# Batch normalisation over 512 MB: the first tile's split moved from a half to a quarter of its columns

## The chip, the cores and the metric

The kernel runs on one core of a Trainium2 chip. Its time is the device time of one execution in microseconds; where several runs were made, the median stands for them. One profiled execution gives the trace from which all details are read. Lower is better.

## The reference

```python
eps = 1e-5
mean = running_mean.reshape(1, -1, 1, 1)
var = running_var.reshape(1, -1, 1, 1)
gamma = gamma.reshape(1, -1, 1, 1)
beta = beta.reshape(1, -1, 1, 1)
return gamma * (x - mean) / np.sqrt(var + eps) + beta
```

`x` is 32 x 256 x 128 x 128 in fp32, 537 MB; the four parameter vectors have one value for each of the 256 channels. The output has the size of `x`. So the kernel reads 537 MB, writes 537 MB, and does one multiplication and one addition for each element.

## The kernel before

A tile is one image's block of 128 channels: 128 partitions by 128 x 128 = 16384 columns, 64 KiB a partition, 8 MB in all. There are 64 tiles (32 images by 2 channel blocks), and three buffers of that size in SBUF that the tiles take in turn. Each tile is computed in place: a load brings it in, VectorE multiplies by a scale and adds a shift for each partition (line 122), a store takes it out.

Three queues of instructions set the order of the work, all written out by hand.

- SyncE (SP) issues all loads. First the left part of tile 0 (line 84), then the four parameter vectors (line 87), then the right part of tile 0 (line 91), then tiles 1 to 63 whole (line 94). The loads of tiles 1 and 2 wait for nothing. From tile 3 on the load of tile i waits until the store of tile i - 3 has landed, since it takes that buffer.
- VectorE first turns the parameters round and works out scale and shift (lines 99 to 117; one square root of it is on ScalarE, line 107). Then it computes tile 0 in two pieces, each when its part has landed (lines 135 and 136), and tiles 1 to 62 in one piece each (line 139). Of the last tile it computes 9216 columns (line 143), and ScalarE the other 7168 beside it (line 145).
- ScalarE (ACT) issues the stores (line 133), one for each tile, when `done` says that the tile is computed. Store 0 waits for both pieces of tile 0.

Loads and stores of a tile have 128 rows of 64 KiB, one a partition. In SP's queue nothing stands between one tile's load and the next, and in ACT's queue, after the parameters' square root, there are only the stores and the last tile's piece of computation.

Of the kernel before, what the change touches and what calls it, by code (L numbers as in the profile page):

```python
# [1 line left out]

# [4 lines left out]


NBUF = 3

VCOLS = 9216


@with_exitstack
def kernel(
    ctx: ExitStack,
    tc: tile.TileContext,
    x: bass.AP,
    gamma: bass.AP,
    beta: bass.AP,  # L20
    running_mean: bass.AP,
    running_var: bass.AP,
    out: bass.AP,
):
    nc = tc.nc
    eps = 1e-5
    f32 = mybir.dt.float32

    N, C, H, W = x.shape
    P = nc.NUM_PARTITIONS  # L30
    assert C % P == 0
    NCB = C // P
    HW = H * W
    NT = N * NCB
    B = 32
    NQ = P // B
    NE = 16
    NPAR = 4

    xr = x.rearrange("n (cb p) h w -> (n cb) p (h w)", p=P)  # L40
    outr = out.rearrange("n (cb p) h w -> (n cb) p (h w)", p=P)

    params = ctx.enter_context(tc.tile_pool(name="params", bufs=1))
    data = ctx.enter_context(tc.tile_pool(name="data", bufs=1))
    bufs = [data.tile([P, HW], f32, name=f"t{s}", tag=f"t{s}") for s in range(NBUF)]
    rows = params.tile([B, NPAR * C], f32, name="rows", tag="rows")
    turned = params.tile([B, NPAR * C], f32, name="turned", tag="turned")
    par = params.tile([P, NPAR, NCB], f32, name="par", tag="par")
    eps_t = params.tile([P, 1], f32, name="eps_t", tag="eps")
    std_t = params.tile([P, NCB], f32, name="std_t", tag="std")  # L50
    rstd_t = params.tile([P, NCB], f32, name="rstd_t", tag="rstd")
    scale_t = params.tile([P, NCB], f32, name="scale_t", tag="scale")
    ms_t = params.tile([P, NCB], f32, name="ms_t", tag="ms")
    shift_t = params.tile([P, NCB], f32, name="shift_t", tag="shift")

    loaded = [tc.alloc_semaphore(f"loaded{s}") for s in range(NBUF)]
    stored = [tc.alloc_semaphore(f"stored{s}") for s in range(NBUF)]
    early = tc.alloc_semaphore("early")  # L60
    done = tc.alloc_semaphore("done")
    fetched = tc.alloc_semaphore("fetched")
    vec = tc.alloc_semaphore("vec")
    act = tc.alloc_semaphore("act")

    with tc.tile_critical():  # L66
        count = [0]

        def step(inst, sem=None, value=None):

            if sem is not None:
                inst._wait_ge(sem, value)
            elif count[0]:
                inst._wait_ge(vec, count[0])
            inst.then_inc(vec, 1)
            count[0] += 1
            return count[0]

        left, right = slice(0, HW // 2), slice(HW // 2, HW)
        last = NT - 1  # L80

        nc.sync.dma_start(out=bufs[0][:, left], in_=xr[0][:, left]).then_inc(early, 16)
        zeroed = step(nc.vector.memset(rows[:], 0.0))  # L85
        for r, ap in enumerate((running_var, gamma, beta, running_mean)):
            inst = nc.sync.dma_start(out=rows[0:NE, r * C : (r + 1) * C], in_=ap.partition_broadcast(NE))  # L87
            if r == 0:
                inst._wait_ge(vec, zeroed)
            inst.then_inc(fetched, 16)  # L90
        nc.sync.dma_start(out=bufs[0][:, right], in_=xr[0][:, right]).then_inc(loaded[0], 16)
        for i in range(1, NT):
            s, turn = i % NBUF, i // NBUF
            inst = nc.sync.dma_start(out=bufs[s][:], in_=xr[i]).then_inc(loaded[s], 16)
            if turn:
                inst._wait_ge(stored[s], 16 * turn)


        step(nc.vector.memset(eps_t[:], eps))  # L99
        step(nc.vector.transpose(out=turned[:], in_=rows[:]), fetched, 16 * NPAR)  # L100

        blocks = turned.rearrange("p (rc q b) -> p rc q b", q=NQ, b=B)
        flat = par.rearrange("p r cb -> p (r cb)")
        for q in range(NQ):
            placed = step(nc.vector.tensor_copy(out=flat[q * B : (q + 1) * B], in_=blocks[:, :, q, 0]))  # L105
        var_t, gamma_t, beta_t, mean_t = (par[:, r] for r in range(NPAR))
        nc.scalar.activation(  # L107
            out=std_t[:],
            in_=var_t,
            func=mybir.ActivationFunctionType.Sqrt,  # L110
            bias=eps_t[:],
            scale=1.0,
        )._wait_ge(vec, placed).then_inc(act, 1)
        step(nc.vector.reciprocal(out=rstd_t[:], in_=std_t[:]), act, 1)  # L114
        step(nc.vector.tensor_mul(out=scale_t[:], in0=gamma_t, in1=rstd_t[:]))  # L115
        step(nc.vector.tensor_mul(out=ms_t[:], in0=mean_t, in1=scale_t[:]))  # L116
        ready = step(nc.vector.tensor_sub(out=shift_t[:], in0=beta_t, in1=ms_t[:]))  # L117
        nc.vector.wait_ge(vec, ready)

        def compute(i, cols=slice(0, HW)):  # L120
            t, cb = bufs[i % NBUF], i % NCB
            return nc.vector.tensor_scalar(  # L122
                out=t[:, cols],
                in0=t[:, cols],
                scalar1=scale_t[:, cb : cb + 1],
                scalar2=shift_t[:, cb : cb + 1],
                op0=mybir.AluOpType.mult,
                op1=mybir.AluOpType.add,
            ).then_inc(done, 1)

        def store(i, after):
            s = i % NBUF
            nc.scalar.dma_start(out=outr[i], in_=bufs[s][:])._wait_ge(done, after).then_inc(stored[s], 16)  # L133

        compute(0, left)._wait_ge(early, 16)
        compute(0, right)._wait_ge(loaded[0], 16)
        store(0, 2)
        for i in range(1, last):
            compute(i)._wait_ge(loaded[i % NBUF], 16 * (i // NBUF + 1))
            store(i, i + 2)  # L140

        turns = last // NBUF + 1
        compute(last, slice(0, VCOLS))._wait_ge(loaded[last % NBUF], 16 * turns)
        t, cb = bufs[last % NBUF], last % NCB
        nc.scalar.activation(  # L145
            out=t[:, VCOLS:],
            in_=t[:, VCOLS:],
            func=mybir.ActivationFunctionType.Identity,
            bias=shift_t[:, cb : cb + 1],
            scale=scale_t[:, cb : cb + 1],  # L150
        )._wait_ge(loaded[last % NBUF], 16 * turns).then_inc(done, 1)
        store(last, last + 3)

        for s in range(NBUF):
            nc.sync.wait_ge(stored[s], 16 * ((NT - s + NBUF - 1) // NBUF))


# [1 line left out]
_INS = ['x', 'gamma', 'beta', 'running_mean', 'running_var']  # L159
_OUTS = [((32, 256, 128, 128), 'float32')]  # L160


# [23 lines left out]
```

## Time and profile before

| What | Value |
|---|---|
| Median of 5 runs | 2507.07 us |
| The five runs | 2515.58, 2483.45, 2509.15, 2483.73, 2507.07 us |
| The profiled execution | 2514.05 us |
| Its span, first to last instruction | 2512.3 us |
| VectorE busy | 564.0 us, 22% |
| DMA, mean over the span | 427 GB/s |
| Read and written | 536.94 MB and 536.87 MB |
| A tile on VectorE (16384 columns) | 8.81 us |
| Half of tile 0 on VectorE (8192 columns) | 4.55 us |
| Store 0 issued | 28.3 us after the start |
| Last store issued, and its time to landing | 2489.8 us, 20.7 us |

The page of a profile lists each engine's busy time, and then the span in 40 equal slices, each with a digit for the busy share in tenths. A line of a group or of the timeline reads: start, duration, engine, line of the code, operation, output<-inputs, shapes; in square brackets the time that the engine stood idle before it and what ended that. A letter q after an engine's name (SPq, ACTq) marks the queue that issues transfers; the time that such an issue takes is not the transfer's. "DMA to landing" is from the issue until the whole transfer has arrived. q1 and q10 are the DMA queues of loads and of stores.

### The profile page before, as it was taken

To read this page: it belongs to the slowest core of one execution; us is meant where nothing else is said; L and a number is where in the kernel's file an instruction comes from. 1 tells how busy PE (TensorE), PEld (TensorE's weight loads), DVE (VectorE), ACT (ScalarE), POOL (GpSimd) and SP (SyncE) were. 2 spreads that over 40 slices of the span, in tenths; PEclk is the share of its full clock that TensorE was granted. 3 is DMA by queue.
4 is the path that set the end of the run, shared out by engine and by line. 5 is a ranking of instruction groups with operands and counts; after the bars stand their busy time and mean duration, and the time that the engine had idled before them with its cause. 6 is when DMAs were issued, how large, how long until landed. Compare 5 with 4: busy or idle time off the path is not lost.

```text
span 2512.3 us, 266 instructions
## 1 busy us (share of the span) xinstructions
DVE 564.0 (22%) x76; ACT 7.9 (0%) x3; POOL 0.2 (0%) x4
## 2 busy tenths in 40 slices
DVE  3121221212212122121221212212222121221221
ACT  0000000000000000000000000000000000000001
POOL 0000000000000000000000000000000000000000
DMA  9999999999999999999999999999999999999997
GB/s 418 432 430 434 434 431 431 433 434 430 432 434 428 432 430 429 431 425 434 429 427 431 432 429 433 428 429 433 433 423 426 426 430 422 428 429 433 430 433 334
DMA packets 18707, 1073.84 MB, mean 427 GB/s; under 512 B 2128, under 2 KB 2192, under 8 KB 2192
## 3 DMA queue, kind: packets, MB, share of 16 engines
q1 hardware_dynamic: 9488, 536.94, 50.0%
q10 hardware_dynamic: 9216, 536.88, 49.6%
q14 instruction: 3, 0.02, 0.0%
HBM read 536.94 MB, written 536.87 MB: 427 GB/s over the span
## 4 chain that ended last, share of the span: by engine, by line
another core or an unknown queue 76%; DVE 22%; DMA 1%; ACT 0%; issue 0%; SPq 0%; ACTq 0%; DVEq 0%
DVE t L122 22%; DMA t<-in_x_dram 1%; ACT t L145 0%; SPq L87 0%; DVE rows L85 0%; ACTq L133 0%; DVE eps_t L99 0%; DVEq L181 0%; SPq L66 0%
## 5 line engine op out<-in xcount | busy, mean ns | idle before, releaser
L122 DVE TENSOR_SCALAR t<-t,scale_t,shift_t 128x16384 f32<-128x16384 f32 (+2 forms) x65 | 560.5, 8624 | 1910.3 <-DMA t<-in_x_dram 1910.1
L145 ACT ACTIVATE t<-t,shift_t,scale_t 128x7168 f32<-128x7168 f32 x1 | 6.4, 6361 | 2466.5 <-DMA t<-in_x_dram 2466.5
L100 DVE STREAM_TRANSPOSE turned<-rows 32x1024 f32<-32x1024 f32 x1 | 1.2, 1233 | 12.3 <-DMA rows<-in_running_mean_dram 12.3
L107 ACT ACT_TABLE_LOAD x1 | 1.3, 1283 | 0.9 <-SPq L66 0.9
L85 DVE MEMSET rows<- 32x1024 f32 x1 | 0.9, 912 | 1.2 <-SPq L66 1.2
L105 DVE COPY par<-turned 32x8 f32<-32x8 f32 x4 | 0.6, 162 | 0.1
L107 ACT ACTIVATE std_t<-par,eps_t 128x2 f32<-128x2 f32 x1 | 0.3, 295 | 14.4 <-DVE par L105 14.4
L114 DVE RECIPROCAL rstd_t<-std_t 128x2 f32<-128x2 f32 x1 | 0.2, 165 | 0.4 <-ACT std_t L107 0.4
L117 DVE TENSOR_TENSOR shift_t<-par,ms_t 128x2 f32<-128x2 f32 x1 | 0.2, 161 | 0.0
L116 DVE TENSOR_TENSOR ms_t<-par,scale_t 128x2 f32<-128x2 f32 x1 | 0.2, 160 | 0.0
L115 DVE TENSOR_TENSOR scale_t<-par,rstd_t 128x2 f32<-128x2 f32 x1 | 0.2, 160 | 0.0
L170 POOL MEMSET const-bfloat16-1.0<- 128x1 bf16 x1 | 0.1, 101 | 0.0
L170 POOL MEMSET const-uint8-127<- 128x1 uint8 x1 | 0.1, 101 | 0.0
L170 POOL MEMSET const-float32-0.0<- 128x1 f32 x1 | 0.1, 98 | 0.2 <-issue 0.2
L170 POOL MEMSET const-float32-1.0<- 128x1 f32 x1 | 0.1, 98 | 0.0
L99 DVE MEMSET eps_t<- 128x1 f32 x1 | 0.1, 59 | 0.1
## 6 DMA issues: line engine op xcount, KB each, us to landing
t<-in_x_dram SPq DMA_DIRECT2D x2, 4096.0 KB, 16.3
out_dram<-t ACTq DMA_DIRECT2D x64, 45.3
t<-in_x_dram SPq DMA_DIRECT2D x63, 63.3
rows<-in_running_var_dram SPq DMA_DIRECT2D x1, 16.0 KB, 11.2
rows<-in_gamma_dram SPq DMA_DIRECT2D x1, 16.0 KB, 11.1
rows<-in_beta_dram SPq DMA_DIRECT2D x1, 16.0 KB, 10.9
rows<-in_running_mean_dram SPq DMA_DIRECT2D x1, 16.0 KB, 11.0
```

The source lines that it names most:

```text
L85: zeroed = step(nc.vector.memset(rows[:], 0.0))
L99: step(nc.vector.memset(eps_t[:], eps))
L100: step(nc.vector.transpose(out=turned[:], in_=rows[:]), fetched, 16 * NPAR)
L105: placed = step(nc.vector.tensor_copy(out=flat[q * B : (q + 1) * B], in_=blocks[:, :, q, 0]))
L107: nc.scalar.activation(out=std_t[:], in_=var_t, func=mybir.ActivationFunctionType.Sqrt, bias=eps_t[:], scale=1.0,)._wait_ge(vec, placed).t ...
L114: step(nc.vector.reciprocal(out=rstd_t[:], in_=std_t[:]), act, 1)
L115: step(nc.vector.tensor_mul(out=scale_t[:], in0=gamma_t, in1=rstd_t[:]))
L116: step(nc.vector.tensor_mul(out=ms_t[:], in0=mean_t, in1=scale_t[:]))
L117: ready = step(nc.vector.tensor_sub(out=shift_t[:], in0=beta_t, in1=ms_t[:]))
L122: return nc.vector.tensor_scalar(out=t[:, cols], in0=t[:, cols], scalar1=scale_t[:, cb : cb + 1], scalar2=shift_t[:, cb : cb + 1], op0=myb ...
L145: nc.scalar.activation(out=t[:, VCOLS:], in_=t[:, VCOLS:], func=mybir.ActivationFunctionType.Identity, bias=shift_t[:, cb : cb + 1], scale ...
L170: nc = _bacc.Bacc("TRN2", target_bir_lowering=False, num_devices=1)
```

## The change

The boundary between tile 0's left and right part goes from column 8192 to column 4096. The left part then has a quarter of the columns (2 MB), the right part three quarters (6 MB). The names `left` and `right` are used by the two loads of tile 0 and by its two computations; nothing else is touched. Store 0 still takes the whole tile after both.

```diff
-        left, right = slice(0, HW // 2), slice(HW // 2, HW)
+        left, right = slice(0, HW // 4), slice(HW // 4, HW)
         last = NT - 1
```

## The prediction

> **What bounds the kernel now.** I read the page first: its DMA lines, then the slices.
>
> ```profile
> DVE 564.0 (22%) x76; ACT 7.9 (0%) x3; POOL 0.2 (0%) x4
> ...
> DMA  9999999999999999999999999999999999999997
> ...
> q1 hardware_dynamic: 9488, 536.94, 50.0%
> q10 hardware_dynamic: 9216, 536.88, 49.6%
> ```
>
> VectorE works 22% of the span, while the loads (q1) and the stores (q10) together fill 99.6% of the time of 16 DMA engines. The chain of waits is of little use here: it books 76% as an unknown queue, which is the time in which the tile loads run. So I went to single tiles. In the order of time VectorE's idle stretch before each tile is the load period less 8.81 us:
>
> ```profile
> 288.95 8.81 DVE L122 TENSOR_SCALAR t<-t,scale_t,shift_t 128x16384 f32<-128x16384 f32 x1 [30.02 <-DMA t<-in_x_dram]
> ...
> 1034.01 8.81 DVE L122 TENSOR_SCALAR t<-t,scale_t,shift_t 128x16384 f32<-128x16384 f32 x1 [30.85 <-DMA t<-in_x_dram]
> 1074.19 8.81 DVE L122 TENSOR_SCALAR t<-t,scale_t,shift_t 128x16384 f32<-128x16384 f32 x1 [31.36 <-DMA t<-in_x_dram]
> ```
>
> An early tile takes 38.8 us, these later ones 39.7 and 40.2. The table of stretches says the same for early, middle and end:
>
> ```profile
> 94.58:366.42 271.84, 61.68 (x7) 0.00 (x0) 0.00 (x0) 1.00 1.00 433
> 366.42:2444.39 2077.97, 467.05 (x53) 0.00 (x0) 0.00 (x0) 1.00 1.00 430
> 2475.00:2490.00 15.00, 5.08 (x1) 6.36 (x1) 0.00 (x0) 1.00 0.27 118
> ```
>
> Columns: stretch, length, VectorE, ScalarE and GpSimd busy, clock, DMA share, GB/s. Seven tiles at 38.83 us, then 53 at 39.21 us. In the third row most DMA engines have run out of work, and a few slow ones still bring in the last tile.
>
> **The floor.** In the trace's packet records a 64 KiB row takes 2.418 us at the median on its DMA engine. Each of 16 engines has 64 tiles x 8 rows x 2 directions = 1024 rows: 2476.0 us. Some 2.5 us at the start, 2 us at the end and 1.7 us around the span (2514.05 less 2512.3) make 2482. The two fastest of the five runs, 2483.45 and 2483.73 us, are practically there; the other three (2507 to 2516) and the profiled one carry about 30 us of packets over 2.418 us on the slowest engine. There are two regimes, and the clean one has been seen with the kernel as it is.
>
> **What tells the regimes apart.** A store is issued when its tile is computed; the previous store is then still running. How long it runs on I call the reserve of the store queue. From single store issues with their landings: store 0 is issued at 28.3 and lands 44.2 later, at 72.5; store 1 is issued at 64.4, so the reserve is 8.1 us.
>
> ```profile
> L133 ACTq DMA_DIRECT2D out_dram<-t x1: 374/374/374, 28.3 to 28.3; - x1
> DMA to landing us min/median/max: 44.2/44.2/44.2
> ...
> L133 ACTq DMA_DIRECT2D out_dram<-t x1: 338/338/338, 64.4 to 64.4; - x1
> DMA to landing us min/median/max: 47.3/47.3/47.3
> ```
>
> Worked the same way it is 8.3 at store 2, 7.6 at store 9, 6.6 at store 10, and from store 15 to the end between 5.6 and 7.2, with 5.6 again and again as its lowest. While it is over 7.5 the stores land every 38.7 us; after that tiles take 39.2. The landing is that of the slowest engine: fast engines end the old store some 4 us earlier, so at a reserve of 5.6 their rings are close to empty before the new store's packets are there.
>
> [...] the packet records, strung end to start into 16 sequences (they name no engine), mostly alternate between loads and stores. [...] The rows of 8192 and 16384 columns (4546 and 8812 ns) give 0.521 ns a column[...].
>
> **The change part by part.** Instructions, bytes and semaphores stay in number. The left load goes from 4 to 2 MB, the right one from 4 to 6; rows of 32 KiB become 16 and 48 KiB, two a partition as before.
>
> Parameters: their four loads are behind the left load in SP's queue and landed at 14.5, right after it (13.8). With 2 MB less ahead at some 430 GB/s they land about 4.9 us earlier, near 9.6. From there the transpose to the last small operation takes 3.2 us and the left computation 8812 - 12288 x 0.521 = 2.41 us: done by about 15.5 instead of 22.3. Nothing waits for that, since the right load lands at 23.7 as before (the same bytes ahead of it). Worth nothing; if the cover were gone it would cost at most the 2.4 us.
>
> Right computation: 12288 columns, 4.546 + 4096 x 0.521 = 6.68 us in place of 4.54. Store 0 is issued at 23.75 + 6.68 = 30.45, 2.13 us later than now. ACT's queue has nothing but later stores behind it. VectorE's next work is tile 1 at 55 us. The DMA engines do not idle: loads 1 and 2 were issued at 4.4 and 4.9 us, and the load queue runs alone for those 2.13 us. Direct cost: nothing.
>
> Phase: in 2.13 us alone each engine brings 0.88 more load rows before stores begin to take every second turn. Load 1 therefore lands 2.13 us earlier (53.4), store 1 is issued at 62.3, and store 0 lands 2.13 us later (74.6). The reserve of the store queue goes from 8.1 to 12.4 us. The price is on the load side: load 63 is issued at 2420.0 and load 62 lands at 2444.4, a reserve of 24.4 us, which falls to 20.1. Still plentiful for the slowest engine.
>
> What the reserve is worth: from 94.6 (load 2) to 2483.4 (load 63) there are 61 periods of 39.16 us. At 38.7 they would take 28 us less: 2514.05 - 28 = 2486. Against the median of 2507.07 that is 21 us, 0.8%. Early on the reserve shrank by 0.1 us a tile, then lost 1 us at one tile; from 12.4 there is room for that several times over. At the tail, the last store now starts when VectorE and ScalarE are done (2489.8), about when store 62 is (2490.6); with the larger reserve store 62 sets this alone, worth within 0.5 us either way.
>
> Unknown is whether reserve causes the regime or shows it. Bound on the good side: the floor, 2482. On the bad side there is no row for other phases between reads and writes; the worst single periods here are 40.2 us. I take the clean stretch's period.
>
> **The rivals.** (1) The reserve is only a symptom: slow read packets put the slowest engine back, whatever the phase. For it: at tile 10 the late load came before the small reserve, and several engines were slow at once. Then the regime falls as before, mostly 2502 to 2516, about 2508. (2) It helps for a time: from store 2 to 15 the reserve fell 0.21 us a tile, so 12.4 lasts some 28 tiles before 6.6 in place of 8; 20 tiles at 0.46 us are 9 us: 2498. (3) Slower: the smaller load reserve. In those sequences the fastest engines finish their loads near 2456, some 27 us ahead of the slowest: more than the 24.4 us of load reserve, so they already wait at the issue of line 94. With 20 us this begins at a smaller lead; engines then run dry and start again together, and first packets of a tile, where most of the slow packets lie, collide more. If that doubles the excess of 0.46 us a tile it costs 28 us, 2535 to 2542; if all periods become the worst seen it is 65 us. It decides once the lead passes 20 us. Against it: the early engines are level. (4) The change doesn't move the store: excluded but for a reserve that steps in whole packets (0 or 4.8 us), which ends in rival 1.
>
> **How the numbers follow.** The clean regime (2482 to 2490, forecast 2486): 0.43. Partial help (2490 to 2502): 0.20. No help (2502 to 2516): 0.20. Slower (2516 and up): 0.17, of which 0.13 past 2532. One per cent, about what a measurement of this kernel can tell from no change, is 25 us: 2482.0 and 2532.1. The floor lies at the first, so faster by over 1% gets 0.08, all from the clean regime; same 0.79; slower 0.13. The range 2481 to 2518 leaves out little but the slower rival.
>
> **What would show it.** Store 0 issued at 30.4 to 30.5; load 1 landed near 53.4; a reserve of 12 to 13 us at store 1, which stays above 7.5; idle stretches before VectorE's tiles of 29.8 to 30.1 all along; some 433 GB/s in the middle stretch. If the reserve is large and the periods are still 39.2 us, my cause is wrong and rival 1 holds. If the reserve has gone back to 5.6 by half way, rival 2. If periods pass 39.5 us on average and engines go idle before 2400 us, rival 3.

## The result, and the profile after

The changed kernel takes 2506.31 us, the median of 28 runs (2483.08 to 2509.45); the kernel before, beside it, 2502.07 us (47 runs, 2483.42 to 2525.60). The ratio is 1.0014, with a 95% interval of 0.9993 to 1.0036: no change. (Ratios, here and below, weigh the runs of both kernels; they are not those of the medians.) The profiled execution has a span of 2498.9 us (2500.64 with what lies around it).

So 2486 was wrong, and rival 1 (no help, about 2508) is what happened. Yet nearly every step on the way to it came as forecast. The order of time at the start, changed kernel (start, length, instruction, idle time before it):

```profile
23.81 6.68 DVE L122 TENSOR_SCALAR t<-t,scale_t,shift_t 128x12288 f32<-128x12288 f32 x1 [8.75 <-DMA t<-in_x_dram]
30.52 31.51 ACTq L133 DMA_DIRECT2D out_dram<-t  x2
52.84 8.81 DVE L122 TENSOR_SCALAR t<-t,scale_t,shift_t 128x16384 f32<-128x16384 f32 x1 [22.36 <-DMA t<-in_x_dram]
```

The right part takes 6.68 us, store 0 is issued at 30.5, load 1 has landed at 52.8. The first two stores, one issue each:

```profile
L133 ACTq DMA_DIRECT2D out_dram<-t x1: 376/376/376, 30.5 to 30.5; - x1
...
DMA to landing us min/median/max: 44.6/44.6/44.6
...
L133 ACTq DMA_DIRECT2D out_dram<-t x1: 339/339/339, 61.7 to 61.7; - x1
...
DMA to landing us min/median/max: 52.6/52.6/52.6
```

Store 0 lands at 75.1, store 1 is issued at 61.7: a reserve of 13.4 us, where 12.4 was worked out. Counted like this, from landings, it also stays. The page's list of transfers gives the median time of a store to its landing:

```profile
t<-in_x_dram SPq DMA_DIRECT2D x1, 6144.0 KB, 19.8
t<-in_x_dram SPq DMA_DIRECT2D x1, 2048.0 KB, 7.5
out_dram<-t ACTq DMA_DIRECT2D x64, 49.8
```

49.8 us, against 45.3 before, over all 64 stores; half way, store 28 is issued at 1116.3 and lands 49.4 later, 10.5 us after store 29's issue. But the tiles are not clean for it:

```profile
286.01 8.81 DVE L122 TENSOR_SCALAR t<-t,scale_t,shift_t 128x16384 f32<-128x16384 f32 x1 [31.07 <-DMA t<-in_x_dram]
...
1029.59 8.81 DVE L122 TENSOR_SCALAR t<-t,scale_t,shift_t 128x16384 f32<-128x16384 f32 x1 [30.31 <-DMA t<-in_x_dram]
```

Idle stretches of 31.07 and 30.31 us, so periods of 39.9 and 39.1, with a reserve of 10 to 14 us. From load 2 (91.4 us) to load 63 (2467.5) the mean period is 38.95 us in this run, which is one of the faster ones; before it was 39.16, and clean is 38.7. A large reserve without clean tiles is what the prediction had named as the sign that its cause is wrong.

The reserve itself says less than it seems to. Each of these transfers leaves 16 landing marks in the trace, and VectorE starts a tile 0.02 to 0.03 us after the last mark of its load (all 63 tiles loaded whole, changed kernel): a landing is that of the slowest engine, and hides what the other 15 have left. The packet records show that too: I count the rows of earlier stores that no engine had begun when a store was issued, and call them waiting rows; a store has 128.

| Store | Kernel before | Changed kernel |
|---|---|---|
| 1 | 11 | 27 |
| 2 to 13 | 6 or 7 | 27, then 19 |
| 14, 15 | 1 | 19, 17 |
| 16 to 62 | 1 to 5 | 2 to 10 |

So the change did bring more waiting rows, but they were gone by store 16 while the reserve by landing still read 10 us: it was that of a few engines. Of the 16 marks of store 15, 12 lie 3.4 to 3.9 us after the issue of store 16, the last one 10.7. Nor were tiles clean while the rows lasted: the period of 39.9 us above falls between store 6, with 27 waiting rows, and store 7, with 19.

In the two profiles the packet records say where the time is. I sum, over all 64 KiB packets after 60 us, what each took beyond 2.418 us, and divide by 16: 22.5 us before (16.2 of it loads), 8.1 after (6.0 loads). I call this sum the excess. The profiled run after has the smaller excess, but strung end to start into 16 sequences it lies on few engines: four or five of them carry some 13 to 25 us each, most of the others 2 to 7. In the run before, all 16 carry between 17 and 29. A tile is computed after the last of its 16 marks, so the largest of these sets the span: 2476 + 4.5 + 18 to 25 is its 2498.9 within the errors of stringing the records together.

### The profile page after: what moved, and what is told of

Same layout as the page of the kernel before. It is cut to its first block, busy times and chain, and to the rows that moved or that the text cites. A ratio compares the mean times of both kernels' runs of the same rounds, so it can differ in the third digit from the quotient of the medians.

```text
span 2498.9 us, 266 instructions
## 1 busy us (share of the span) xinstructions
DVE 564.0 (23%) x76; ACT 7.9 (0%) x3; POOL 0.2 (0%) x4
## 4 chain that ended last, share of the span: by engine, by line
another core or an unknown queue 75%; DVE 22%; DMA 2%; ACT 0%; issue 0%; SPq 0%; ACTq 0%; DVEq 0%
DVE t L122 22%; DMA t<-in_x_dram 2%; ACT t L145 0%; SPq L87 0%; DVE rows L85 0%; SPq L91 0%; ACTq L133 0%; DVE eps_t L99 0%; DVEq L181 0%; SPq L66 0%
## 6 DMA issues: line engine op xcount, KB each, us to landing
out_dram<-t ACTq DMA_DIRECT2D x64, 49.8
```

## The experiments

In the expectations R is the prediction's theory (the reserve holds the clean regime). S, M, B, W, H and P are rivals that came up on the way. "Near the floor" means under 2488 us. The kernel before was run beside every experiment: 45 of its 194 runs in all lay near the floor, 51 over 2510. It has a broad distribution, so ratios and shares count here, not single times. The diffs show the lines that matter and leave the others out.

**More reserve, less reserve.**

```diff
 # e1_late: split at a quarter; the right part on ScalarE
-        compute(0, right)._wait_ge(loaded[0], 16)
+        on_act(0, right)._wait_ge(loaded[0], 16)
 # e2_early: tile 0 in three loads; its last quarter on both engines
+        compute(0, third)._wait_ge(second, 16)
+        compute(0, on_dve)._wait_ge(loaded[0], 16)
+        on_act(0, on_sca)._wait_ge(loaded[0], 16)
```

> The split at a quarter, and the right three quarters of tile 0 computed on ScalarE in place of VectorE: 12288 columns at 0.887 ns (6361 ns for 7168) are 10.9 us, so store 0 is issued near 34.7 us, 6.4 us later than in the kernel before, and the reserve of the store queue at store 1 is some 8.1 + 2 x 6.4 = 21 us. Theory R (the reserve holds the clean regime; the quarter split gave too little of it): nearly all runs at 2483 to 2486. Theory S (a DMA engine that has fallen behind the others pays some 0.5 us at the first row of each of its loads, whatever the reserve): no change, median 2498 to 2508, with single runs at 2484.

Measured: 2504.70 us (21 runs, 2499.74 to 2511.39), ratio 1.0022 (1.0000 to 1.0044). Its first two stores (here the line is 143):

```profile
L143 ACTq DMA_DIRECT2D out_dram<-t x1: 376/376/376, 34.1 to 34.1; - x1
...
DMA to landing us min/median/max: 43.1/43.1/43.1
...
L143 ACTq DMA_DIRECT2D out_dram<-t x1: 339/339/339, 57.0 to 57.0; - x1
```

Store 0 lands at 77.2, so the reserve is 20.2 us at store 1; until the last store it is never under 20. Not one of 21 runs lay near the floor. The profiled run's excess was 13.0 us. R, as the prediction measured the reserve, is refuted. That was not a full store queue on every engine, though: 62 rows were waiting at store 1, and from store 16 on only 4 of 128.

> Tile 0 comes in three loads (half, quarter, quarter), and its last quarter is computed by VectorE and ScalarE together: 2048 columns take 1.35 us and 1.9 us, so store 0 is issued near 26.1 us, 2.2 us earlier than in the kernel before, and the reserve at store 1 is near 3.7 us in place of 8.1. R: the clean regime is gone from the start, no run below 2490, median 2510 to 2520. S: no change, median 2498 to 2508.

Measured: 2509.50 us (14 runs, 2483.67 to 2523.81), ratio 1.0017 (0.9984 to 1.0051). Store 0 was issued at 25.9, the reserve was 0.8 us at store 1, 5.6 a tile later, and between 5.5 and 7.8 from there on: the small reserve that R's forecast rests on lasted for one tile. One run, not the profiled one, lay near the floor. So a reserve of 6 or of 20 us gives the same time within 0.5%.

**Is it VectorE, or engines out of step?**

```diff
 # e3_load_step: a load waits for the load before it as well
+            if turn:
+                nc.sync.wait_ge(loaded[(i - 1) % NBUF], 16 * ((i - 1) // NBUF + 1))
 # e4_no_compute: lines 122 and 145 left out, a store waits for its load
-            compute(i)._wait_ge(loaded[i % NBUF], 16 * (i // NBUF + 1))
-            store(i, i + 2)
+            nc.scalar.dma_start(out=outr[i], in_=bufs[s][:])._wait_ge(loaded[s], 16 * (i // NBUF + 1)).then_inc(stored[s], 16)
```

> From tile 3 on the load of a tile is issued only when the load before it has landed on all 16 DMA engines, so that every engine begins each load together with the others; nothing else changes. S: no engine can stay behind on loads, the slow first rows are gone, and since the stores fill the gap between two loads the time is 2483 to 2490. R: the store reserve is what it is before or less, no gain: 2500 to 2512. [...]

Measured: 2512.61 us (21 runs, 2506.13 to 2517.14), ratio 1.0033 (1.0012 to 1.0054). In the trace all 16 sequences now lie near the mean excess of 23.8 us; none is behind, and all are equally slow. S's forecast failed: an engine need not lag to be slow. But the edit did more than level the engines. From load 3 and store 2 on, at every issue, no row of its queue was left waiting on any engine, and 15 of the 23.8 us lie in the load packet just ahead of a store's first, the place that e16_every_second shows below. So this run doesn't tell what lagging does in the kernel before.

> The multiplication and addition of all tiles are left out (the parameters are still worked out): a store waits for its tile's load alone, and the output is x. The 8.8 us between landing and store go, so store 0 is issued near 23.8 us and the reserve at store 1 is small (0 to 4 us). If VectorE's accesses to SBUF are what slows the packets, the time is 2483 to 2486. R: small reserve, no clean regime: 2510 to 2520. S: no change, 2498 to 2508.

Measured: 2500.26 us (21 runs, 2483.65 to 2515.71), ratio 0.9981 (0.9953 to 1.0009), 4 of 21 runs near the floor, as often as the kernel before. VectorE is not the cause: with all 64 tiles of computation taken away the time stays within 0.5%.

**Loads alone, stores alone.**

```diff
 # e5_loads_only
-                inst._wait_ge(stored[s], 16 * turn)
+                inst._wait_ge(done, i - NBUF + 2)
-            store(i, i + 2)
+            if i >= NT - NBUF:
+                store(i, i + 2)
 # e6_stores_only
-        for i in range(1, NT):
+        for i in range(1, NBUF):
```

> All 64 tiles are loaded and computed, but only the last three are stored; a load waits for the computation of the tile three before it. 512 + 24 rows a DMA engine at 2.418 us are 1296 us, with the start, the end and what lies around the span a floor near 1302. Theory M (slow packets come from loads meeting stores): reads alone are clean, 1300 to 1305 in all runs and next to no packet over 2.45 us. Theory L (each load pays for itself, 15 to 30 us over 504 rows in the profile of before): 1317 to 1332, with a spread of 20 us.

> Three tiles are loaded and computed, and then stored again and again to all 64 places; the other 61 loads and computations are left out. The same floor, near 1302. M: 1300 to 1305 in all runs. If stores alone are slowed, 1310 or more; the stores' share of the slow packets was the smaller one before (6.9 of 25.3 us), so I expect none.

Measured: 1305.32 us (4 runs, 1304.96 to 1305.42) and 1308.59 us (4 runs, 1308.40 to 1310.55). The excess is 1.9 us over 493 load rows an engine, and 3.0 over 508 store rows, most of it 4 ns a row (the median row takes 2.422 us in both). The stores come out 3 to 5 us over M's 1300 to 1305. Still, both directions are nearly clean alone, and they repeat within 0.5 and 2.2 us where the whole kernel spreads over 40. The many slow packets need loads and stores at one time.

**Twice as many transfers.**

```diff
 # e7_loads_halved (e8_stores_halved: the same at line 133)
+            for rows_ in (slice(0, P // 2), slice(P // 2, P)):
+                inst = nc.sync.dma_start(out=bufs[s][rows_], in_=xr[i][rows_]).then_inc(loaded[s], 16)
 # e9_two_parts: columns instead, big = 12288, small = 4096, loads and stores
+            nc.sync.dma_start(out=bufs[s][:, big], in_=xr[i][:, big]).then_inc(loaded_a[s], 16)
+            nc.sync.dma_start(out=bufs[s][:, small], in_=xr[i][:, small]).then_inc(loaded[s], 16)
 # e10_turns: e9_two_parts, and the two directions take turns
+                nc.sync.wait_ge(stored_a[(i - 2) % NBUF], 16 * ((i - 2) // NBUF + 1))
+                nc.scalar.wait_ge(loaded_a[(i + 1) % NBUF], landed_a(i + 1))
```

> Each load of tiles 1 to 63 is issued as two, of 64 partitions each; rows keep their 64 KiB, an engine gets 4 rows from each. Theory B (the first row of a transfer[...] costs the 0.4 us a tile): twice as many transfers, twice the excess, median 2520 to 2535 and no run under 2495. M (a matter of how reads and writes of the engines fall together in time, the transfer's bounds play no part): 2498 to 2510, with single runs near 2484.

> The same for the stores: two issues of 64 partitions for each tile. B, if it is a store's issue that slows the load packets beside it: 2520 to 2535. M: 2498 to 2510.

Measured: 3381.03 us (6 runs, 3287.41 to 3497.02; the kernel before beside it 2508.61) and 2988.39 us (6 runs, 2955.13 to 3006.90, ratio 1.1888). Far outside both theories, so they don't test B. The stretch from 500 to 1500 us of the first moved 320 GB/s:

```profile
500.00:1500.00 1000.00, 167.43 (x19) 0.00 (x0) 0.00 (x0) 1.00 0.99 320
```

The engines were busy 99% of it; a load row took 4.05 us in the mean in place of 2.42. What makes rows of half the partitions slower no run here shows.

> Loads and stores of tiles are each issued as two transfers over all 128 partitions, of 12288 and 4096 columns (rows of 48 and 16 KiB); order and waits stay. B (each transfer's start costs): the excess of 0.4 us a tile doubles, median 2520 to 2535, none under 2495. M (slow packets come where loads and stores meet, not at a transfer's bounds): the excess stays, and 1024 more packets an engine at some 8 ns (two rows of 32 KiB took 2.426 us, one of 64 KiB 2.418) add 8 us: median 2506 to 2518, with single runs near 2491.

> The same two parts, and loads and stores take turns: the store of tile i waits until the first part of load i + 1 has landed, and load i + 2 waits until the first part of store i has landed, so that the two meet only while a second part (some 5 us of 19) runs. M: loads and stores almost never meet, few slow packets, a narrow spread: 2490 to 2496 in all runs. If the meeting isn't the cause: as e9_two_parts. [...]

Measured: 2579.40 us (6 runs, 2493.83 to 2610.76) and 2535.10 us (6 runs, 2518.78 to 2543.77; ratio 1.0142, 1.0089 to 1.0196). With two transfers in place of one the excess in the profile was 58 us, 2.6 times that of before: B's direction, but more than the doubling and the 2520 to 2535 us that it forecast. And one run came in at 2493.83, 4 us over its floor of 2490, where B had none under 2495; so not every transfer's start costs. Taking turns didn't make it clean: the excess was 49 us with engines busy throughout, and the slow packets lie within about 4 us after an issue. M as I had put it (few meetings, few slow packets) is refuted.

**Other places in HBM.**

```diff
 # e11_one_source: every load from line 94 reads tile 0
-            inst = nc.sync.dma_start(out=bufs[s][:], in_=xr[i]).then_inc(loaded[s], 16)
+            inst = nc.sync.dma_start(out=bufs[s][:], in_=xr[0]).then_inc(loaded[s], 16)
```

> Loads of tiles 1 to 63 all read the first tile of x again (the output is wrong for it; every other step stays), so the places in HBM that loads and stores touch at one time stand in another relation. Theory H (slow packets are a matter of which places of HBM are read beside which are written): the distribution changes, to all runs near 2484 or to a median over 2520. If places play no part: as the kernel before, 2500 to 2510 in the median with single runs at 2484.

Measured: 2493.29 us (22 runs, 2483.31 to 2515.01), ratio 0.9990 (0.9959 to 1.0021), 9 of 22 near the floor beside 9 of 27 of the kernel before. H is refuted for the reading side. Its profiled execution was a clean one, 2484.36 us with a span of 2482.6, and an excess of 1.4 us. Stores 48 and 49 of it, and the tile between them:

```profile
L133 ACTq DMA_DIRECT2D out_dram<-t x1: 338/338/338, 1883.0 to 1883.0; - x1
...
DMA to landing us min/median/max: 46.0/46.0/46.0
...
1912.75 8.81 DVE L122 TENSOR_SCALAR t<-t,scale_t,shift_t 128x16384 f32<-128x16384 f32 x1 [29.83 <-DMA t<-in_x_dram]
...
L133 ACTq DMA_DIRECT2D out_dram<-t x1: 338/338/338, 1921.6 to 1921.6; - x1
```

The period is 38.64 us, clean, at a reserve of 7.3 us and with 5 waiting rows of 128. So neither a reserve over 7.5 us nor a full store queue is needed for clean tiles.

**Small stores.**

```diff
 # e12_small_stores
-            nc.scalar.dma_start(out=outr[i], in_=bufs[s][:])._wait_ge(done, after).then_inc(stored[s], 16)
+            nc.scalar.dma_start(out=outr[i][:, cols], in_=bufs[s][:, cols])._wait_ge(done, after).then_inc(stored[s], 16)
 # cols = 0:4096; e13_small_stores_2: 0:2048 and 8192:10240, after each half's computation
```

> All tiles are loaded and computed, but of each tile only the first 4096 columns are stored, in one transfer (128 rows of 16 KiB); the other three quarters of the output are left out. The store queue is empty between two stores, the load queue never. 512 x 2.418 + 64 x 8 x 0.611 us = 1551, with the start and an uncovered end near 1570. Theory W (an issue into an empty queue holds up the packets in flight, 0.3 to 0.6 us an engine as after each issue when the queues took turns): some 0.4 us a tile of slow load packets, 25 us in the sum over an engine, 1590 or more. M (loads are slow in proportion to the store packets they meet): a quarter of the 16 to 18 us of before, 4 to 5 us, near 1575.

> The same bytes stored, but in two transfers of 8 KiB rows for each tile, each issued after the computation of its half, some 4 us apart, so that both find the queue empty. W: twice the slow load packets of e12_small_stores. M: as many as there.

Measured: 1561.64 us in both runs, and 1589.92 and 1590.48 us. The order of time of the first:

```profile
804.78 48.66 ACTq L133 DMA_DIRECT2D out_dram<-t  x3
...
820.10 8.81 DVE L122 TENSOR_SCALAR t<-t,scale_t,shift_t 128x16384 f32<-128x16384 f32 x1 [15.35 <-DMA t<-in_x_dram]
844.26 8.81 DVE L122 TENSOR_SCALAR t<-t,scale_t,shift_t 128x16384 f32<-128x16384 f32 x1 [15.36 <-DMA t<-in_x_dram]
```

Tile after tile takes 24.16 us, and the excess of the whole run is 0.1 us: 64 tiles with as many store packets as load packets and hardly a slow one. So the meeting as such cost no more than that, even for full load rows. A store took 27.4 us to land (8 load rows and 8 short packets of an engine are 8 x (2.418 + 0.611) = 24.2 us), 3.2 us after the next was issued. By its rows, though, the store queue was empty at all but one issue: none was waiting. So issues into a store queue just emptied cost no more than that 0.1 us with rows of 16 KiB, against W.

The second has as many bytes in twice the transfers and 24.6 us of excess, all of it loads. It did not do what its expectation says: at three of four store issues some 110 to 230 store rows were still waiting, and it was the load queue that had none left at every second load's issue, which never happened in the first.

**Issues into an empty queue.**

```diff
 # e15_every_second_small: 0:4096 of every second tile; e16_every_second: all of it
-            store(i, i + 2)
+            if i % 2 == 0:
+                store(i, i + 2)
```

> As e12_small_stores, but only every second tile is stored (4096 columns of it); the rest of the output is left out. In e12_small_stores the store queue had turned out never to be empty (a store of 8 rows an engine lasts as long as a load of 8 rows); here a store meets one load, and during the next load the store queue is empty, so each of 32 stores is issued into an empty queue while loads run on. 1238 + 32 x 8 x 0.611 = 1394, with start and end near 1400. W (an issue into an empty queue holds up the load packets): 0.3 to 0.6 us for each of 32 issues, 10 to 19 us of excess an engine. If an empty queue doesn't matter: under 1 us, as in e12_small_stores.

> Every second tile is stored, whole (rows of 64 KiB); the other half of the output is left out. 512 + 256 rows at 2.418 us are 1857, with start and end near 1863. W: 10 to 19 us of excess an engine. M (size of the store's packets, which e12_small_stores had at a quarter): half of the 16 us of before, 8 us, spread over the time in which a store runs. Neither: under 2 us, and then the slow packets need both queues to be full at once for long.

Measured: 1404.42 us (2 runs) with 0.4 us of excess, and 1907.73 us (2 runs, 1905.29 and 1910.16) with 35.0 us. So W's effect is there with rows of 64 KiB and not with rows of 16, though both find the store queue empty for 18 to 19 us. Its size was forecast at 10 to 19 us; 24 of the 35 lie in the one load packet ahead of a store's first, 0.8 us for each store and engine. In the second, one store is issued at 1038.4; stretches ahead of it, right after it, and later:

```profile
1029.00:1038.40 9.40, 8.81 (x1) 0.00 (x0) 0.00 (x0) 1.00 1.03 446
1038.40:1043.00 4.60, 0.00 (x0) 0.00 (x0) 0.00 (x0) 1.00 1.00 285
1043.00:1057.00 14.00, 0.00 (x0) 0.00 (x0) 0.00 (x0) 1.00 0.99 431
```

The last column but one is the DMA share, the last GB/s: after the issue the engines are as busy as ever and start 285 GB/s. On 14 of the 16 engines the load packet that runs when the store begins takes 3.6 to 4.1 us in place of 2.42.

**The changed kernel again, and a split between the two.**

```diff
 # e17_three_eighths (e14_after_again is the changed kernel)
-        left, right = slice(0, HW // 2), slice(HW // 2, HW)
+        left, right = slice(0, 3 * HW // 8), slice(3 * HW // 8, HW)
```

> The changed kernel once more, for its distribution beside the kernel before on the same chip. If the larger reserve does no good: median within 0.3% of the kernel before, and, as the first 28 runs had it, fewer runs than before both under 2488 and over 2510. If the first distribution was chance: about a quarter of the runs under 2488, as before.

> The split at three eighths: the right part is 10240 columns, 5.61 us, store 0 is issued 1.07 us later than in the kernel before and 1.06 earlier than in the changed one; the reserve is near 10 us. If clean runs grow rarer with a larger reserve (25% of the runs under 2488 at 8 us, 8% at 13, none of 21 at 20): some 10 to 20% of the runs under 2488, median 2500 to 2506. If the reserve has nothing to do with it: as the kernel before on the same chip.

Measured: 2504.37 us (8 runs, 2501.45 to 2507.42), ratio 1.0056 (1.0025 to 1.0088), none near the floor while 6 of 13 runs of the kernel before were; and 2516.35 us (16 runs, 2503.49 to 2530.36), ratio 1.0065 (1.0035 to 1.0094), none near the floor. The changed kernel thus has 3 of 36 runs near the floor and none over 2510: a narrower distribution at the same median over its first 28 runs. The three-eighths kernel has no clean run either, but is slow otherwise: 13 of 16 over 2510. In its profile the reserve was 8.2 us at store 1, not the 10 expected but that of the kernel before. So neither the share of clean runs nor the time follows the reserve. Where store 0 falls does move the distribution by some tenths of a per cent; I have no rule for how.

**Shorter rows, order and waits as before.**

```diff
 # e18_rows_32k: three of its sixteen lines
-    bufs = [data.tile([P, HW], f32, name=f"t{s}", tag=f"t{s}") for s in range(NBUF)]
+    bufs = [data.tile([P, 2, HW // 2 + 16], f32, name=f"t{s}", tag=f"t{s}") for s in range(NBUF)]
-            inst = nc.sync.dma_start(out=bufs[s][:], in_=xr[i]).then_inc(loaded[s], 16)
+            inst = nc.sync.dma_start(out=bufs[s][:, :, half], in_=xr[i]).then_inc(loaded[s], 16)
-            nc.scalar.dma_start(out=outr[i], in_=bufs[s][:])._wait_ge(done, after).then_inc(stored[s], 16)
+            nc.scalar.dma_start(out=outr[i], in_=bufs[s][:, :, half])._wait_ge(done, after).then_inc(stored[s], 16)
```

> Each buffer row has a gap of 64 bytes in its middle, so that a transfer moves two rows of 32 KiB a partition in place of one of 64; transfers, order and waits stay (the last tile's VectorE piece is two instructions). A row of 32 KiB took 1.213 us, so the floor is 2482 + 1024 x 0.008 = 2490. Theory P (a packet is held up by the long row that another queue brings in: 64 KiB rows 1.1 us a store in e16_every_second, 16 KiB rows nothing in e15_every_second_small and e12_small_stores): shorter rows, shorter hold-ups, most runs at 2490 to 2496 and a narrow spread, which beats both kernels by 0.3 to 0.6%. If the length of the row doesn't matter: the spread of the kernel before on top of 8 us, 2491 to 2528, median near 2512.

Measured: 2486.47 us, 6 runs from 2486.17 to 2487.42; the kernel before beside it 2508.10 (11 runs, 2496.30 to 2519.05). The ratio is 0.9917, 0.9892 to 0.9943. Page and stretches of this kernel (the same two as in the prediction, cut short before the end):

```profile
DMA packets 34963, 1073.84 MB, mean 432 GB/s; under 512 B 2128, under 2 KB 2192, under 8 KB 2192
...
q1 hardware_dynamic: 17552, 536.94, 50.1%
q10 hardware_dynamic: 17408, 536.88, 50.0%
```

```profile
94.58:366.42 271.84, 62.55 (x8) 0.00 (x0) 0.00 (x0) 1.00 1.00 433
366.42:2390.00 2023.58, 464.56 (x53) 0.00 (x0) 0.00 (x0) 1.00 1.00 433
```

```profile
1022.04 8.81 DVE L122 TENSOR_SCALAR t<-t,scale_t,shift_t 128x16384 f32<-128x16384 f32 x1 [29.90 <-DMA t<-in_x_dram]
1060.75 8.81 DVE L122 TENSOR_SCALAR t<-t,scale_t,shift_t 128x16384 f32<-128x16384 f32 x1 [29.90 <-DMA t<-in_x_dram]
1099.47 8.81 DVE L122 TENSOR_SCALAR t<-t,scale_t,shift_t 128x16384 f32<-128x16384 f32 x1 [29.91 <-DMA t<-in_x_dram]
```

Nearly twice the packets, the same bytes, 433 GB/s from the first stretch to the last, and idle stretches that repeat to 0.01 us. The excess of the whole run is 0.1 us, against 22.5 in the kernel before with the same order and waits. P's narrow spread is there, in all six runs, at 2486 to 2487 us, 4 us below its forecast of 2490 to 2496. The reserve, 9.4 us at store 1, is near that of before, but the waiting rows are not: 43 to 47 of 256 at every store but the last, against mostly 1 of 128. Whether that is what makes the kernel clean or what comes of it, no run tells. It beats both kernels; against the changed one it was not run on the same chip, but 28 + 8 runs of that have medians of 2506.3 and 2504.4.

## Why the prediction was wrong

By its own steps:

- The bound and the floor held. A clean run exists at the time worked out: 2484.36 us in the profile of e11_one_source, and 2482.5 to 2484 in the fastest runs of the kernel before, against 2482.
- The right computation (6.68 us), store 0 at 30.45, load 1 at 53.4 held: 6.68, 30.5 and 52.8. The direct cost was nothing, as said. The parameters were ready for the left part at 12.65 us, and it was done at 15.1, where 15.5 was forecast; its 4096 columns took 2.41 us, as worked out, so the 0.521 ns a column measured at 8192 and 16384 held at both new widths. Loads and stores do mostly alternate: strung into 16 sequences, 84% of the packets from 60 to 2400 us before and 76% after follow one of the other direction. The reserve of 12.4 us was 13.4 at store 1 in the first profile and 10.4 in the second, and stayed above the 7.5 us that it was to stay over.
- The step that failed is "What the reserve is worth", and under it "What tells the regimes apart". I had seen reserve and period move together at one place in one trace, store 9 to 15, and took the first for the cause. With 20 us of reserve none of 21 runs was clean; with 7.3 us a run was (e11), at 38.64 us a tile. And the measure was at fault: from landings it is the slowest engine's reserve. In the trace of before, store 0's 16 marks lie between 69.3 and 72.5 us, and its first packet starts 4.4 us after its issue. The prediction had the fast engines close to empty at a reserve of 5.6 us; by the rows mostly 1 of 128 was waiting there, but only 6 or 7 even in the stretch with 8 us that it took for safe, and the changed kernel was back to 4 by store 16. The gain of 28 us was worked out correctly for a regime that the change doesn't bring.
- "Unknown is whether reserve causes the regime or shows it" was written, and still 0.43 went to the cause and 0.20 to rival 1. The evidence for rival 1 that the text itself named (the late load came before the small reserve, and on several engines at once) should have weighed more. The five runs were a second sign: two of them at the floor with nothing in the kernel changed.
- Rival 2 forecast a gain that lasts as long as the reserve. By landings the reserve lasted, by waiting rows it was gone at store 16; the time shows no gain either way. Rival 3's price never came due: the load reserve fell to 19.4 us for most of the run and to 16.4 at load 63, more than the 20.1 forecast, and the time did not rise.
- In place of the failed step the runs put this. The time over the floor is slow packets, added up on the slowest engine. They take both directions (e5, e6), and neither VectorE (e4) nor the place read (e11) makes them. One case was shown directly: a store of 64 KiB rows issued into a queue that had been empty for 18 us slowed a load packet on nearly every engine by 1.2 to 1.7 us (e16); with 16 KiB rows the excess of the whole run was 0.4 us (e15). And the kernel with rows of 32 KiB is clean (e18). That slow packets of the kernel before are of that same kind is argued, not shown.

What stays open. e18 also spaced the buffers by 128 bytes more in each partition, and has some 45 waiting rows at each store; I did not run a kernel with the spacing alone, nor one with long rows and a store queue kept filled on all engines. That row length is the lever is the reading that e15 and e16 support. e13 doesn't fit a rule by the store's row alone: its stores had rows of 8 KiB, and the full load rows beside them were slow by 24.6 us, with a load queue that ran empty. Nor does e9, whose rows of 48 and 16 KiB had 58 us. What a lagging engine costs is open too, since e3 emptied both queues. Why a run of the kernel before is clean or not, with nothing changed, is not explained, nor why three other places of store 0 (3/8, 1/4, late) gave hardly any clean runs: 0 of 16, 3 of 36 and 0 of 21.

## What to carry to other kernels

When single runs of one unchanged kernel already reach the floor, the question is what differs between runs; a quantity that an edit can move is a cause only when moving it, alone and far, moves the time. Check too what the quantity measures: a reserve read from landings was that of the slowest of 16 engines. For a kernel whose loads and stores keep the DMA engines busy throughout, count the packets that take longer than the usual one and see which engine has the most: the mean share of 99.6% hid 30 us. And try shorter rows in the same transfer before tuning phases: here sixteen changed lines gave 0.8%, though the row length is not told apart from the buffers' spacing.

## What the runs showed of the hardware that I had not expected

- A transfer's rows are its packets (16256 records of 64 KiB before, for 127 transfers of 128 rows): at the median 64 KiB took 2.418 us, 32 KiB 1.213, 16 KiB 0.611, 8 KiB 0.309. Two half rows take 8 ns more than a whole one, by that sum 8 us here; measured, the kernel with short rows is some 3 us over the clean runs of the kernel before (2482.5 to 2484), and 21.6 us under its median beside it (2508.1 - 2486.5).
- A store's landing hides how little is left: at a reserve of 20 us, 4 of its 128 rows were waiting (e1).
- Splitting a 128-partition transfer into two of 64 partitions made the kernel 31 to 39% (loads) or 18 to 20% (stores) slower; with the loads split, the DMA engines were busy 99% of the stretch from 500 to 1500 us.
- One unchanged kernel spread over 2482.5 to 2531.5 us in 194 runs, loads alone over 0.5 us in 4, and the kernel with short rows over 1.3 us in 6.
